# The recurrence's values in one job of 512 columns, attention outputs by way of DRAM, and a first scaling on two engines

## The chip, the core and the metric

The kernel runs on one core of a Trainium2 chip: TensorE (PE) multiplies and writes to PSUM, VectorE (DVE), ScalarE (ACT) and GpSimd (POOL) work element by element, SyncE (SP) issues loads, and each engine runs its own instructions in order, held by semaphores. The metric is the device time of one execution in microseconds, as the median of several runs. The profile is one further execution.

## The reference

One layer of a streaming encoder on x of 1024 tokens x 1024 channels, all in float32:

```
xn = rmsnorm(x, norm1_g);  u = xn @ w_in
q,k,v (8 heads of 64), f,i,q,g (4 heads of 128), gates a,b (1024 each) = split(u)
attention:   w_ts = sigmoid(z_ts) * prod_{s<j<t} (1 - sigmoid(z_tj));   o_sb = w @ v
recurrence:  S_t = diag(f_t) S_{t-1} + k_t i_t^T;  o_t = S_t^T silu(q_t);  o_hg = rmsnorm(o) * silu(g)
merged = sigmoid(a) * (o_sb @ w_o_sb) + sigmoid(b) * (o_hg @ w_o_hg)
h = x + merged @ w_out;  h += relu(rmsnorm(h) @ w_ff1)^2 @ w_ff2;  out = rmsnorm(h)
```

What the change touches are the columns `i` of w_in (512: the values of the recurrence, 128 for each of its four heads), the attention output o_sb, and the scaling inside the first rmsnorm.

## The kernel before

**Two parts for each operand.** Products of float32 accuracy are made of three matmuls (`three`, line 526): each operand is split into a high part (a cast on ScalarE, `hi_copy`, line 143) and a low part (a subtraction on VectorE, `lo_sub`, line 146), and high x high, high x low and low x high are added in PSUM. A weight piece of 128 x 1024 is loaded by SP into one of two buffers with the tag "raw", then split (`Unit.load` and `Unit.split`, lines 435 to 461); the raw buffer comes free with its split. All loads go through SP in one fixed order (`load`, line 128).

**Fill and main.** TensorE's order is written out by two lanes (lines 89 to 118). The main lane holds the attention, and later the recurrence, whose steps depend on VectorE and ScalarE. Between its steps lie steps of "fill": projections out of a stream of jobs (`Stream`, line 471), which need only xn and a weight. A job of a projected head half is 24 matmuls of 512 columns; one step is 6 of them. When a job starts, the weights of the next are split and those of the one after are loaded (`prefetch`, line 490).

**Projections with tokens on the partitions.** The attention's values and the recurrence's values are made by `token_steps` (line 552) from `wide_unit` (line 575): 256 columns of w_in in two pieces of 128 x 1024 (4 k-tiles of 256 columns each), 8 token blocks x 8 k-tiles x 3 matmuls of 256 columns. `i_job(h)` (line 886) makes so the values of heads h and h+1 (`wi0`, `wi2`, PSUM name `pji0`, `pji2`) and ScalarE copies each head's 128 columns out. It is called from `hg_jobs` (line 917) for heads 0 and 2. So the stream holds, behind the last q and k of the attention: f0, q0, i of heads 0 and 1, g0, f1, q1, g1, raw block 0 (gates), f2, q2, i of heads 2 and 3, g2, and so on. For its first job the prefetch is put off to the seventh step and behind a certain cast (`late`, `hi_behind`).

**Attention.** For each head and block of 128 queries: score product `z`, sigmoids on ScalarE, a scan and a product on VectorE (`weights`, line 767), transposes `pw` with their split (`turn`, line 791), and for each pair of blocks the product with v (`values`, line 831, PSUM name `po`), added into `osb`, one SBUF slot of 128 x 1024 for each pair of heads. Of the fill, `n_fill` = 126 steps are spread over it; they end two steps into f1. The four `osb` slots are held from there until the last gate blocks (`raw_job`, line 1276 on), where they are split for the output projection.

**Recurrence.** Heads are treated one after the other by levels: VectorE forms running products of the decay `pp` with `k` and `q`, ScalarE and VectorE split them, TensorE multiplies (`sd`, `sl`), with fill steps between. The rate of fill is a list of constants by stage.

**Start.** `first_norms` (line 596) norms x's first token blocks: ScalarE and VectorE each square half the columns, GpSimd makes the inverse root (line 248), VectorE scales the whole block of 128 x 1024 (line 615), TensorE transposes it (`xnt`) and the first projection `pjqk` begins.

Of the kernel before, what the change touches and what calls it, by code (L numbers as in the profile page):

```python
# [19 lines left out]
P = 128  # L20
# [19 lines left out]
def kernel(  # L40
# [43 lines left out]
    def bank(name):  # L84
        return psum.tile([P, 512], F32, tag="p", name=name)

    class Lane:
        def __init__(self):  # L90
# [458 lines left out]

        return st.add([u for _, u, _ in group], body)  # L550

    def token_steps(name, unit, acts, tbs, epilogue, lo_last=False):

        for tb in tbs:
            ps = bank(f"{name}_{tb}")[:, 0:256]
            for lo in (False, True) if lo_last else (None,):
                for kt in range(KT):
                    sh, sl = acts.stat(kt, tb)
                    wh, wl = unit.hl[kt // 4]
                    cs = slice((kt % 4) * 256, (kt % 4 + 1) * 256)  # L560
# [12 lines left out]
            yield  # L573

    def wide_unit(name, mat, c0):
        return Unit(
            name,
            [
                [
                    (  # L580
                        0,
                        256,
                        mat[k * 512 : (k + 1) * 512, c0 : c0 + 256].rearrange(
                            "(k p) c -> p k c", p=P
                        ),
                    )
                ]
                for k in range(2)
            ],
            wide=True,  # L590
        )
# [4 lines left out]
    def first_norms(tbs):  # L596
        (l, lc), (r, rc) = halves()
        means = {}
        for tb in tbs:
            t, scr = xt[tb], slot(f"n1scr{tb}")  # L600
            ssq = small.tile([P, 1], F32, tag="ssq1", name=f"n1_{tb}_ss", bufs=4)
            in_turn(
                "act",
                nc.scalar.activation(
                    scr[:, lc], t[:, lc], AF.Square, scale=D ** -0.5, accum_out=ssq
                ),
            )
            ms = mean_square(scr[:, rc], t[:, rc], EPS, f"n1_{tb}")
            in_turn("dve", add(ms, ms, ssq))
            means[tb] = inv_root(ms, f"n1_{tb}")  # L610
        for tb in tbs:
            t = xt[tb]
            in_turn(
                "dve",
                nc.vector.tensor_scalar(
                    out=t, in0=t, scalar1=means[tb], scalar2=None, op0=ALU.mult
                ),
            )
            if tb == tbs[0]:
                turn_vectors(0, 1)  # L620
        for part in range(2):
            u_qk0.split(part)
# [168 lines left out]
    def turn(h, qb, between):  # L791
# [36 lines left out]
        seen[h, qc] = seen.get((h, qc), 0) + 1  # L828
        return (h, qc) if seen[h, qc] == 2 else None

    def values(h, qc):
# [25 lines left out]


    hg, ohg = {}, {}
# [23 lines left out]

        return ep

    def i_job(h):
        unit = wide_unit(f"wi{h}", W_IN, C_I + h * P)

        def ep(ps, tb):
            for j in range(2):  # L890
                if tb == 0:
                    hg[h + j, "v"] = slot(f"v{h + j}")
                nc.scalar.copy(hg[h + j, "v"][:, tb * P : (tb + 1) * P], ps[:, j * P : (j + 1) * P])

        unit.late = h == 0

        def body():
            for i, _ in enumerate(token_steps(f"pji{h}", unit, xn, range(NT), ep)):
                yield
                if unit.late and i == 6:  # L900
                    hi_behind[0] = turn_hi[0]
                    st.prefetch()
                    hi_behind[0] = None

        return st.add([unit], body)

    def silu_epilogue(h, key):
        def ep(ps, half):
# [3 lines left out]

        return ep

    j_hg = {}

    def hg_jobs(h):
        for key, c0, ep in (
# [7 lines left out]
            j_hg[h] = proj_jobs([(f"pj{key}{h}", u, ep)], xn)  # L926

    hg_jobs(0)

# [149 lines left out]
    def hg_tail(h):  # L1079
# [5 lines left out]
        for half in range(2):  # L1085
# [67 lines left out]
    class Split:  # L1153
# [15 lines left out]

    a_sb, a_hg = Split("asb"), Split("ahg")  # L1170
    mgs = Acts("ms")
    scratch = ctx.enter_context(
        tc.tile_pool(name="scratch", bufs=1, space=bass.MemoryType.DRAM)
    )

    def dram(name, shape):
        return scratch.tile(shape, F32, tag=name, name=name)

    def half(name, dt=F32):
        return hpool.tile([P, 512], dt, tag="h", name=name)  # L1180

# [74 lines left out]
    def raw_job(cb):  # L1256
# [13 lines left out]
        def body():  # L1270
            p1, p14, g1 = (half(f"{n}_{cb}") for n in ("p1", "p14", "g1"))
            ps, p4 = bank(f"pga{cb}"), bank(f"pgq{cb}")
            if cb >= 6:
                load_g1(cb - 6)
            yield from steps_of(ps, 0, 0, 0, 0, True)
            hi_behind[0] = nc.scalar.copy(p1, ps)
            nc.scalar.dma_start(pd[cb][:, 0, :], p1)
# [11 lines left out]
            (nc.gpsimd if cb < 6 else nc.scalar).dma_start(gd[cb], g1)  # L1289
            if cb >= 4:  # L1290
                a_sb.put(cb - 4, osb[cb - 4])

        return st.add([u], body)

# [86 lines left out]

    j_raw = []
    hg_jobs(1)
    j_raw.append(raw_job(0))
    hg_jobs(2)
    j_raw.append(raw_job(1))
# [777 lines left out]
    for i, it in enumerate(items):  # L2164
# [150 lines left out]
```

## Time and profile before

| | |
|---|---|
| median of 3 runs | 1444.71 us (1444.4 to 1445.86) |
| the profiled execution | 1444.02 us |
| its span in the profile | 1442.2 us |
| TensorE / VectorE / ScalarE / GpSimd busy | 1431.7 / 1105.9 / 664.4 / 142.4 us |

The profile page shows busy time by engine, the span in 40 slices, the DMA queues, the chain of work that ended last, and the costliest groups of instructions. Further views of the same trace are quoted below: the waits of an engine (total us, times, longest), the busy table of chosen windows, the chain inside a window (start us, length us, what), the timeline of an engine (start us, length us, then engine, line, operation), groups by shape (count | busy us, mean ns | idle before), and DMA issues with the median time from issue to landing. Line numbers are those of the kernel before. Matmuls overlap in the trace: the distance from one to the next is its price, not its duration.

### The profile page before, as it was taken

The numbers are of one execution on the slowest core, as the hardware profiler recorded it, in microseconds if no ns is written. First come the engines' busy times: TensorE is split into PE (matmuls) and PEld (weight loads), VectorE is DVE, ScalarE is ACT, GpSimd is POOL, SyncE is SP. The second block draws the span as 40 slices with busy tenths as digits, with TensorE's granted clock in tenths as the row PEclk, the third lists the DMA queues.
The fourth block names the chain that finished last, engine by engine and source line by source line (L and its number), as shares of the span: only waits on it lengthen the run. The fifth ranks groups of instructions, "written<-read, shape, count | busy, mean of one in ns | idle before, by whom it ended". The sixth has DMA issues, their size and how long they took to land.

```text
span 1442.2 us, 19976 instructions
## 1 busy us (share of the span) xinstructions
PE 1431.7 (99%) x7464; PEld 1220.0 (85%) x7464; DVE 1105.9 (77%) x1583; ACT 664.4 (46%) x1150; POOL 142.4 (10%) x338
## 2 busy tenths in 40 slices
PE   9999999999999999999999999999999999999998
PEld 8989988988898888888888888888888888888886
DVE  7699899798747788878778898666666757768765
ACT  7566666652323244432335574444444433523343
POOL 3121121110000012100000300000000000000042
PEclk9999999999999999999999999999999999999999
DMA  7234154321303249655487415344445974776725
GB/s 213 48 98 104 37 96 82 59 44 51 99 21 103 70 134 247 228 177 174 145 292 251 159 46 191 122 144 158 157 150 207 350 262 173 261 276 245 275 100 185
DMA packets 157369, 224.68 MB, mean 156 GB/s; under 512 B 25644, under 2 KB 93784, under 8 KB 157272
## 3 DMA queue, kind: packets, MB, share of 16 engines
q1 hardware_dynamic: 143128, 184.86, 38.0%
q0 software_dynamic: 11264, 33.56, 9.1%
q10 hardware_dynamic: 2880, 4.98, 0.9%
q8 instruction: 59, 0.97, 0.3%
q14 instruction: 38, 0.31, 0.1%
HBM read 162.03 MB, written 61.34 MB: 155 GB/s over the span
## 4 chain that ended last, share of the span: by engine, by line
PE 94%; DVE 3%; issue 1%; ACT 1%; POOL 1%; DMA 0%; SPq 0%; DVEq 0%; POOLq 0%; ACTq 0%
PE pm L121 21%; PE pX L121 9%; PE pW L121 6%; PE pY L121 6%; PE pjqk L121 6%; PE pji L121 3%; PE pys L121 3%; PE pga L121 3%; PE pyh L121 3%; PE gY L121 3%; PE gX L121 3%; PE pjg L121 2%; PE po L121 2%; PE pjv L121 2%; PE z L121 2%; PE pjf L121 2%
## 5 line engine op out<-in xcount | busy, mean ns | idle before, releaser
L144 ACT CAST whid<-w 128x1024 fp32r<-128x1024 f32 x30 | 31.6, 1053 | 152.3 <-PE pm L121 84.4
L777 DVE TENSOR_TENSOR_SCAN rm<-rm,bits 128x511 f32<-128x511 f32 (+7 forms) x72 | 87.3, 1220 | 14.2 <-ACT rm L755 12.7
L121 PE MATMUL pm<-wlod,sh 128*128 128x512 f32 x240 | 93.5, 390 | 0.0
L121 PE MATMUL pm<-whid,sh 128*128 128x512 f32 x240 | 93.4, 389 | 0.0
L121 PE MATMUL pm<-whid,sl 128*128 128x512 f32 x240 | 93.4, 389 | 0.0
L121 PE MATMUL pm<-tl,sh 128*128 128x512 f32 (+1 forms) x210 | 81.3, 387 | 0.0
L121 PE MATMUL pm<-th,sl 128*128 128x512 f32 (+1 forms) x210 | 81.3, 387 | 0.0
L121 PE MATMUL pm<-th,sh 128*128 128x512 f32 (+1 forms) x210 | 81.3, 387 | 0.0
L149 DVE TENSOR_TENSOR wlod<-w,whid 128x1024 fp32r<-128x1024 f32 x30 | 36.7, 1223 | 55.4 <-ACT whid L144 55.4
L149 DVE TENSOR_TENSOR sl<-sa,sh 128x1024 fp32r<-128x1024 f32 x56 | 68.3, 1219 | 1.4 <-ACT sh L144 1.4
L144 ACT CAST wTh<-pw 128x128 fp32r<-128x128 f32 (+3 forms) x96 | 44.4, 487 | 51.0 <-PE pw L124 43.5
L144 ACT CAST sh<-sa 128x1024 fp32r<-128x1024 f32 x56 | 57.3, 1047 | 7.4 <-DMA sa<-ad 7.4
L1957 POOL TENSOR_SCALAR fss<-fss 128x1 f32<-128x1 f32 x8 | 4.5, 560 | 562.2 <-ACT fsc L1952 561.6
L149 DVE TENSOR_TENSOR wTl<-pw,wTh 128x512 fp32r<-128x512 f32 (+3 forms) x96 | 50.8, 548 | 8.7 <-ACT wTh L144 6.0
L121 PEld LDWEIGHTS pm<-wlod,sh 128*128 128x128 f32 x240 | 45.1, 188 | 10.0 <-DVE wlod L149 0.4
L121 PEld LDWEIGHTS pm<-whid,sl 128*128 128x128 f32 x240 | 45.1, 188 | 9.3
L157 DVE TENSOR_TENSOR bt<-bt,rm 128x511 f32<-128x511 f32 (+7 forms) x72 | 48.9, 686 | 5.1 <-ACT bt L758 1.0
L121 PEld LDWEIGHTS pm<-whid,sh 128*128 128x128 f32 x240 | 45.0, 187 | 9.3
L121 PE MATMUL pX<-sql,t1h 128*128 128x512 f32 x128 | 50.0, 391 | 0.1
L121 PE MATMUL pX<-sqh,t1h 128*128 128x512 f32 x128 | 49.9, 389 | 0.0
L121 PE MATMUL pX<-sqh,t1l 128*128 128x512 f32 x128 | 49.8, 389 | 0.0
L755 ACT ACTIVATE rm<-z 128x511 f32<-128x511 f32 (+6 forms) x96 | 47.6, 502 | 4.5 <-DVE bt L157 1.9
(927 smaller groups left out, 4592.0 us busy)
## 6 DMA issues: line engine op xcount, KB each, us to landing
w<-in_w_ff_dram SPq DMA_DIRECT2D x72, 512.0 KB, 5.2
sa<-ad SPq DMA_DIRECT2D x56, 512.0 KB, 6.5
ad<-a SPq DMA_DIRECT2D x32, 256.0 KB, 2.0
ad<-s SPq DMA_DIRECT2D x16, 512.0 KB, 5.5
tw<-in_w_out_dram POOLq DMA_DIRECT2D x24, 256.0 KB, 4.0
x<-in_x_dram SPq DMA_DIRECT2D x8, 512.0 KB, 9.0
xnl<-xnh POOLq DMA_DIRECT2D x8, 512.0 KB, 11.8
pr<-pd SPq DMA_DIRECT2D x8, 512.0 KB, 6.3
```

The costliest lines, as they stand in the source:

```text
L121: return pe(nc.tensor.matmul(*a, **k))
L144: hi_last[0] = after(in_turn("act", nc.scalar.copy(dst, src)), hi_behind[0])
L149: nc.vector.tensor_tensor(out=dst, in0=src, in1=hi.bitcast(F32), op=ALU.subtract),
L157: return nc.vector.tensor_tensor(out=out, in0=a, in1=b, op=ALU.mult)
L755: nc.scalar.activation(rm[:, s0 + c0 - 1 : s0 + m - 1], z[:, c0:m], AF.Sigmoid, scale=-0.125)
L777: sc = nc.vector.tensor_tensor_scan(out=rr, data0=rr, data1=bits[:, 1024 - nk + a : 1024 - nk + b][:, ::-1], initial=rm[:, b : b + 1] if i ...
L1957: nc.gpsimd.tensor_scalar(out=ssq, in0=ssq, scalar1=1.0 / D, scalar2=EPS, op0=ALU.mult, op1=ALU.add)
```

## The change

1. `wide_unit` and `token_steps` take a width n. `i_job()` is called once and makes the values of all four heads: 512 columns, four pieces of 128 x 1024 (2 k-tiles of 512 columns each), matmuls of 512 columns, a step after every second k-tile. It is put behind g1, before raw block 0, and finished before the first state product that needs it (`st.finish(j_i)`). Fill in the attention now ends with q1 (125 steps). The late prefetch is gone.
2. When the last values of a head pair are added, GpSimd stores `osb` to DRAM (`od`) and the slot comes free; gate blocks 4 to 7 load it again through SP. The stores of the gates of blocks 2 to 5 go to ScalarE's queue in place of GpSimd's.
3. Of the first token block, ScalarE scales the right half and VectorE the left.

```diff
-    def token_steps(name, unit, acts, tbs, epilogue, lo_last=False):
+    def token_steps(name, unit, acts, tbs, epilogue, lo_last=False, n=256):
+        pk = 1024 // n
         for tb in tbs:
-            ps = bank(f"{name}_{tb}")[:, 0:256]
+            ps = bank(f"{name}_{tb}")[:, 0:n]
...
-                    wh, wl = unit.hl[kt // 4]
-                    cs = slice((kt % 4) * 256, (kt % 4 + 1) * 256)
+                    wh, wl = unit.hl[kt // pk]
+                    cs = slice((kt % pk) * n, (kt % pk + 1) * n)
                     if lo is None:
                         three(ps, sh, sl, wh[:, cs], wl[:, cs], kt == 0, kt == KT - 1)
-                        if kt == 3:
+                        if kt < KT - 1 and kt % pk == pk - 1:
                             yield
...
         for tb in tbs:
-            t = xt[tb]
+            first = tb == tbs[0]
+            if first:
+                t = xt[tb][:, rc]
+                in_turn("act", nc.scalar.activation(t, t, AF.Copy, scale=means[tb]))
+            t = xt[tb][:, lc] if first else xt[tb]
             in_turn(
                 "dve",
                 nc.vector.tensor_scalar(
                     out=t, in0=t, scalar1=means[tb], scalar2=None, op0=ALU.mult
                 ),
             )
...
+        to_come[h] = to_come.get(h, NT // 2) - 1
+        if r and to_come[h] == 0:
+            od[pair] = dram(f"od{pair}", [P, 1024])
+            nc.gpsimd.dma_start(od[pair], osb.pop(pair))
...
-    def i_job(h):
-        unit = wide_unit(f"wi{h}", W_IN, C_I + h * P)
+    def i_job():
+        unit = wide_unit("wi", W_IN, C_I, HGW)
+        vs = []
         def ep(ps, tb):
-            for j in range(2):
+            for h in range(NHG):
                 if tb == 0:
-                    hg[h + j, "v"] = slot(f"v{h + j}")
-                nc.scalar.copy(hg[h + j, "v"][:, tb * P : (tb + 1) * P], ps[:, j * P : (j + 1) * P])
-        unit.late = h == 0
...
+                    vs.append(slot(f"v{h}"))
+                    hg[h, "v"] = vs[h]
+                nc.scalar.copy(vs[h][:, tb * P : (tb + 1) * P], ps[:, h * P : (h + 1) * P])
+        return st.add([unit], lambda: token_steps("pji", unit, xn, range(NT), ep, n=HGW))
...
-            if key == "g" and h % 2 == 0:
-                i_job(h)
...
+        st.finish(j_i)
         open_block("main")
...
+            if cb >= 4:
+                osb[cb - 4] = slot(f"osr{cb}")
+                load(osb[cb - 4], od[cb - 4])
...
-            (nc.gpsimd if cb < 6 else nc.scalar).dma_start(gd[cb], g1)
+            (nc.gpsimd if cb < 2 else nc.scalar).dma_start(gd[cb], g1)
             if cb >= 4:
-                a_sb.put(cb - 4, osb[cb - 4])
+                a_sb.put(cb - 4, osb.pop(cb - 4))
...
     hg_jobs(1)
+    j_i = i_job()
     j_raw.append(raw_job(0))
...
-    n_fill = 9 * (j_hg[0] - j_qk[0]) + 18
+    n_fill = 9 * (j_q[1] - j_qk[0]) + 9
...
-        st.advance(want - done, j_hg[1])
+        st.advance(want - done, j_q[1])
...
-    st.finish(j_hg[0])
+    st.finish(j_q[1])
```

More of the change, by code (lines that the diff above doesn't have):

```diff
@@ L85, in bank, with dram @@
         return psum.tile([P, 512], F32, tag="p", name=name)
+    scratch = ctx.enter_context(
+        tc.tile_pool(name="scratch", bufs=1, space=bass.MemoryType.DRAM)
+    )
+    def dram(name, shape):
+        return scratch.tile(shape, F32, tag=name, name=name)
     class Lane:
@@ L573, in token_steps, with wide_unit @@
             yield
-    def wide_unit(name, mat, c0):
+    def wide_unit(name, mat, c0, n=256):
+        rows = 1024 // n * P
         return Unit(
@@ L578, in wide_unit @@
             [
[L579 to L588, printed above, removed]
+                [(0, n, mat[r : r + rows, c0 : c0 + n].rearrange("(k p) c -> p k c", p=P))]
+                for r in range(0, D, rows)
             ],
@@ L618, in first_norms @@
             )
-            if tb == tbs[0]:
+            if first:
                 turn_vectors(0, 1)
@@ L829, in turn @@
         return (h, qc) if seen[h, qc] == 2 else None
+    to_come, od = {}, {}
     def values(h, qc):
@@ L884, in f_epilogue @@
         return ep
-    def i_job(h):
-        unit = wide_unit(f"wi{h}", W_IN, C_I + h * P)
+    def i_job():
+        unit = wide_unit("wi", W_IN, C_I, HGW)
+        vs = []
         def ep(ps, tb):
-            for j in range(2):
+            for h in range(NHG):
                 if tb == 0:
-                    hg[h + j, "v"] = slot(f"v{h + j}")
-                nc.scalar.copy(hg[h + j, "v"][:, tb * P : (tb + 1) * P], ps[:, j * P : (j + 1) * P])
-        unit.late = h == 0
[L897 to L905, printed above, removed]
+                    vs.append(slot(f"v{h}"))
+                    hg[h, "v"] = vs[h]
+                nc.scalar.copy(vs[h][:, tb * P : (tb + 1) * P], ps[:, h * P : (h + 1) * P])
+            if tb == NT - 1:
+                vs.clear()
+        return st.add([unit], lambda: token_steps("pji", unit, xn, range(NT), ep, n=HGW))
     def silu_epilogue(h, key):
@@ L913, in silu_epilogue @@
         return ep
-    j_hg = {}
+    j_hg, j_q = {}, {}
     def hg_jobs(h):
@@ L922, in hg_jobs @@
         ):
-            if key == "g" and h % 2 == 0:
-                i_job(h)
             u = cols_unit(f"w{key}{h}", [(W_IN, c0 + h * P, P)])
             j_hg[h] = proj_jobs([(f"pj{key}{h}", u, ep)], xn)
+            if key == "q":
+                j_q[h] = j_hg[h]
     hg_jobs(0)
@@ L1171 @@
     mgs = Acts("ms")
[L1172 to L1177, printed above, removed]
     def half(name, dt=F32):
```

## Prediction

> **What bounds the kernel now.** I read the head of the page first (busy shares, clock, chain), then the waits of TensorE, then the chain and the busy table around the places that the change touches.
>
> ```profile
> span 1442.2 us, 19976 instructions
> ...
> PE 1431.7 (99%) x7464; PEld 1220.0 (85%) x7464; DVE 1105.9 (77%) x1583; ACT 664.4 (46%) x1150; POOL 142.4 (10%) x338
> ...
> PEclk9999999999999999999999999999999999999999
> ...
> PE 94%; DVE 3%; issue 1%; ACT 1%; POOL 1%; DMA 0%; SPq 0%; DVEq 0%; POOLq 0%; ACTq 0%
> ```
>
> TensorE is busy for 99% of the span at an even clock. So the time is the sum of what TensorE streams, plus the few places where it stands still. The waits of TensorE name all that a semaphore explains:
>
> ```profile
> PE warm L121 <- POOL ident masks.py:199: 2.2, 1, 2.2
> PE xnt L124 <- DVE x L615: 0.4, 1, 0.4
> PE pjqk L121 <- DVE xnl L325: 0.3, 1, 0.3
> PE sl L121 <- DVE q L157: 0.2, 1, 0.2
> ```
>
> 2.2 us is the fixed start; 0.7 us are the first rows (touched by the change); 0.2 us is in the recurrence of head 0. A change can therefore win only through fewer streamed columns or through these tenths. It can lose more easily, because TensorE is this full only as long as VectorE keeps up. The busy table (first number behind the window: its length; then PE, PEld, DVE, ACT, POOL, clock, DMA share) shows how near VectorE is:
>
> ```profile
> 200.00:254.00 54.00, 54.00 (x309) 46.64 (x308) 50.18 (x73) 34.51 (x77) 10.98 (x38) 1.00 0.44 85
> 254.00:316.00 62.00, 61.79 (x443) 57.79 (x442) 50.27 (x73) 37.47 (x95) 10.34 (x40) 1.00 0.33 58
> 316.00:358.00 42.00, 41.83 (x246) 34.96 (x245) 39.15 (x92) 10.79 (x17) 0.00 (x0) 1.00 0.14 42
> ```
>
> The end of the attention (254 to 316) leaves VectorE 62.00 - 50.27 = 11.7 us idle; the first recurrence stage (316 to 358) only 2.85 of 42. The chain of waits asked for 314 to 358 says the same: start, length, what.
>
> ```profile
> 313.95 1.13 DVE sd_l L149
> ...
> 330.67 1.13 DVE wg1l L149
> ...
> 342.54 0.35 DVE q L157
> 342.93 2.05 PE sl L121 x16
> ```
>
> For 29 us, from 313.95 to 342.93, the chain is VectorE's own (with short gaps), and TensorE hangs on its last product by 0.2 us. That is the place to price.
>
> **Change 1: one job of 512 columns for two of 256.** Counts: the six groups of 256-column matmuls, of which the first and the last are
>
> ```profile
> L121 PE MATMUL pji<-wi0h,xnh x64: 278/283/288, 254.4 to 290.5; 128*128 128x256 f32 x64
> ...
> L121 PE MATMUL pji<-wi2h,xnl x64: 281/283/287, 393.9 to 422.4; 128*128 128x256 f32 x64
> ```
>
> make 6 x 64 = 384. The changed program has 8 token blocks x 8 k-tiles x 3 products = 192 with 512 columns. The durations in these rows overlap (matmuls are pipelined), so the price is the pitch in the chain, pieces without a gap:
>
> ```profile
> 256.84 2.88 PE pji L121 x24
> ...
> 280.12 0.44 PE pw L124 x4
> ```
>
> ```profile
> 610.94 2.72 PE gX L121 x12
> ```
>
> 2.88 / 24 = 0.120 us for 256 columns, 2.72 / 12 = 0.2267 us for 512. TensorE saves 384 x 0.1198 - 192 x 0.2267 = 46.0 - 43.5 = **-2.45 us**, if nothing makes it wait. The Trainium skill (TensorE: Matmul & The Clock Gate, Back-to-back issue gap) gives an isolated gap of N/2.4 + 2.5 ns; by it the saving would be only 384 x 109.2 - 192 x 215.8 ns = 0.5 us and the time 2 us later. The rows above hold some 13 ns beside N/2.4 at both widths, so they disagree with the page, and the sum goes by the rows.
>
> **What moves with it, end of the attention.** The fill work that covers VectorE's attention work is now g of head 0, then f and q of head 1 (3 x 48 matmuls of 512 columns, 144 x 0.2267 = 32.6 us from 254 on). Before it was the values' first job, g of head 0 and 12 matmuls of f (192 x 0.1198 + 60 x 0.2267 = 36.6 us): 4.0 us less cover. VectorE gets the four scalings after f and the two products after q:
>
> ```profile
> L157 DVE TENSOR_TENSOR g<-pjg,g 128x512 f32<-128x512 f32 x2 | 1.4, 698 | 1.2 <-ACT g L910 1.2
> ...
> L149 DVE TENSOR_TENSOR wg1l<-wg1r,wg1h 128x1024 fp32r<-128x1024 f32 x1 | 1.2, 1231 | 0.0
> ...
> L875 DVE TENSOR_SCALAR pp<-pp,oml,lb 128x512 f32<-128x512 f32 x2 | 1.1, 546 | 0.0
> L872 DVE TENSOR_SCALAR k<-k,oml 128x512 f32<-128x512 f32 x2 | 1.0, 478 | 0.0
> ```
>
> The first row stands for such a product, the second for the split of a weight piece. Two each of 0.546 and 0.478 and two products of 0.7 are 3.4 us more. Its idle time there falls from 11.7 to about 11.7 - 4.0 - 3.4 = 4.3 of 58 us. The window 200 to 254 has the same density (3.8 idle of 54) and TensorE stands at 54.00 of 54.00 in it, so I charge only scattered waits: **+0.3** (0 to 1.5). At the very end a cover goes: the values of block 2 of the last head wait for the transposes "pw" to pass ScalarE (high part) and VectorE (low part). Before, 12 matmuls of f (2.7 us) lay between; now only the four transposes of the next block (0.44 us, above).
>
> ```profile
> 312.42 0.59 ACT L144 CAST wTh<-pw 128x512 fp32r<-128x512 f32 x1 [1.08 <-PE pw L124]
> ```
>
> ```profile
> 313.27 0.68 DVE L149 TENSOR_TENSOR wTl<-pw,wTh 128x512 fp32r<-128x512 f32 x1
> ```
>
> 0.59 + 0.68 - 0.44, and 0.1 for handing over: **+0.9** (0.5 to 1.5). Both engines are free for it by then in the changed order, or it is longer.
>
> **First recurrence stage.** I count from the last score product, which ends where this row starts,
>
> ```profile
> 304.04 0.39 PE L121 MATMUL pjg<-xnh,wg0h 128*128 128x512 f32 x1
> ```
>
> to the product at 342.93. TensorE streams 126 fill matmuls of 512 columns there in both programs (before 18 of head 0's g and 48, 48 and 12 of head 1's f, q and g; after 24 of q, 48 of g and 54 of the values), so its time is the same. VectorE's list changes by: four splits of the values' weights (4 x 1.231), two products after g (2 x 0.7) and the next level's full product (1.2) come; one product, two splits, and the four scalings (0.7 + 2.46 + 2.05) go: 7.5 - 5.2 = 2.3 us more. VectorE was the chain here by 0.2 us, and idle for 2.85 us of its window. So TensorE waits for between 0.2 (the gaps take all) and 2.5 us (they take nothing).
>
> A second chain lies in the same place. The weights come in four pieces through two raw buffers: piece 2 is loaded when piece 0 is split, the following gate weights when piece 2 is split. ScalarE, in order, has the casts of pieces 2 and 3, then the gate weights' cast, then the sigmoid after g, then the cast of level 1. The times of these on ScalarE, and L, the time of one load:
>
> ```profile
> L910 ACT ACTIVATE g<-pjg 128x512 f32<-128x512 f32 x2 | 1.2, 598 | 8.6 <-PE pjg L121 8.6
> ...
> L144 ACT CAST wga0whi<-wga0r 128x1024 fp32r<-128x1024 f32 x1 | 1.0, 1043 | 0.0
> ```
>
> ```profile
> wga0r<-in_w_in_dram SPq DMA_DIRECT2D x1, 512.0 KB, 3.8
> ```
>
> ```profile
> wi0r<-in_w_in_dram SPq DMA_DIRECT2D x2, 512.0 KB, 5.5
> ```
>
> From the last score product: piece 0 split at +11.2 (it takes the place of q's weight split, beside `sd_l`, which ends at 315.08), L, cast and split 2.3, L, cast 1.05, sigmoid 0.6, product 0.7, level 1's product 1.2, its cast 1.0: 18 + 2L. TensorE wants it after 86 fill matmuls and 6 others of 0.2267, 20 of 0.12 and 12 transposes of 0.11, 24.6, and the 0.9 above: +25.5. With L = 3.8, the load of this very stage, where the DMA share is 0.14, it comes at 25.6; with 5.5, measured for the same weights while other loads ran, at 29.0. I take 3.8, by which VectorE's own list sets the stage, and of its 0.2 to 2.5 the middle: **+1.35** (0.2 to 4). What stalls TensorE here gives VectorE time back, so the ring and VectorE's excess don't add.
>
> **What goes.** The 0.2 us at 342.93, and what TensorE loses without a named wait at the old end of the attention (62.00 - 61.79 = 0.2 in the window above), are replaced by the new waits: **-0.4** (-0.4 to 0). In head 1's stage the second 256-column job leaves with its splits; VectorE has room there already, so nothing beyond the count.
>
> **Change 2: attention outputs in DRAM.** Four stores of 512 KB from GpSimd behind the last values of a head pair, four loads on SP at gate blocks 4 to 7. Nothing computes on them until the output projection; the load waits for the store, long past, and for a slot. Behind it on SP are the next gate weights; the splits that follow are VectorE's and ScalarE's. Near the last of them the DMA engines are full:
>
> ```profile
> 550.00:580.00 30.00, 30.00 (x196) 25.36 (x195) 23.89 (x45) 13.73 (x33) 9.50 (x13) 1.00 1.05 286
> ```
>
> 0.5 MB at 286 GB/s is 1.8 us later there for what queues behind; TensorE doesn't stand still in that window. I cost it at **0** (-0.3 to +2). The gate stores of blocks 2 to 5 go to ScalarE's queue, where the later blocks' already are:
>
> ```profile
> 552.15 0.33 ACTq L1289 DMA_DIRECT2D gd<-g  x1
> ```
>
> 4 x 0.33 us in an engine 46% busy: 0 (0 to 0.5).
>
> **Change 3: x0's scaling on two engines.**
>
> ```profile
> 5.53 0.56 POOL L248 TENSOR_TENSOR n_y<-n_ms,expo 128x1 f32<-128x1 f32 x1 [3.19 <-DVE n_ms L1183]
> ...
> 6.69 0.74 DVE L615 TENSOR_SCALAR x<-x,n_y 128x1024 f32<-128x1024 f32 x1
> 6.85 0.99 POOL L248 TENSOR_TENSOR n_y<-n_ms,expo 128x1 f32<-128x1 f32 x1 [0.76 <-DVE n_ms L1183]
> 7.10 0.62 ACT L144 CAST wqk0whi<-wqk0r 128x512 fp32r<-128x512 f32 x1 [0.57 <-DMA wqk0r<-in_w_in_dram]
> ...
> 7.88 0.75 DVE L615 TENSOR_SCALAR x<-x,n_y 128x1024 f32<-128x1024 f32 x1 [0.37 <-POOL n_y L248]
> ...
> 10.28 0.38 PE L121 MATMUL pjqk<-xnh,wqk0whi 128*128 128x256 f32 x1 [0.28 <-DVE xnl L325]
> ```
>
> The second root on GpSimd takes 0.99 instead of 0.56 beside VectorE's scaling and ends with it plus the rest of its own. With half the columns on VectorE (0.48 by the row of `k`) it should end some 0.3 earlier, and x1's scaling and the chain to 10.28 with it; ScalarE's half of x0 fits into its 0.57 idle, but pushes the cast at 7.10 by 0.1 to 0.2. **-0.25** (-0.4 to 0). By the Trainium skill (SBUF — State Buffer, SBUF: two separate sides) the two engines hold a port pair exclusively; then the root gains all that VectorE gives up, at most 0.4.
>
> **Sum** on the profiled execution of 1444.0 (span 1442.2 and 1.8 around it): -2.45 + 0.3 + 0.9 + 1.35 - 0.4 + 0 - 0.25 = -0.55, so 1443.5; the median of the runs, 1444.71 (1444.4 to 1445.86), lies 0.7 above that execution, so the forecast is **1444.2**, a change of nearly nothing. The times below are from the median.
>
> **The rivals.** (a) *The full gain*: VectorE's gaps take in every new wait, as they do from 200 to 254. -2.45 - 0.25 - 0.4 = -3.1: 1441.6. Against it stand the 2.3 us more in a stage whose chain is VectorE already. (b) *Slower: the ring of two raw buffers.* Split, load, split, load, cast, sigmoid stand in series in the first recurrence stage; each us of L costs two. From L = 4.1 on it sets the stage (18 + 2L against 25.5 and some 0.7 of VectorE's), and from 4.6 on the kernel is slower than before: 18 + 9.2 - 25.5 = 1.7, with 0.3, 0.9 and 0.2 that is the 3.1 gained. At 5.5 it is 3.5 + 0.3 + 0.9 + 0.2 - 3.1 = +1.8: 1446.5; at 6.3, +3.4: 1448.1. For it: 5.5 is measured for such weights; against: 3.8 in this stage. (c) *VectorE bounds the attention's end and its excess stays whole*: the upper ends, 1.5 + 1.5 + 2.5 - 3.1 = +2.4: 1447.1. (d) *The outputs' round trip*: a load that waits for its slot holds up SP, and gate weights behind it come late by the 1.8 us above: -0.55 + 1.8 = +1.25: 1446.0. (e) *The change doesn't do what it says*, the pitch per column stays that of 256: no saving, -0.55 + 2.45 = +1.9: 1446.6; the two rows nearly exclude it.
>
> **How the numbers follow.** The forecast with its neighbours 50%, (a) 20%, (b) 13%, (c) 10%, (d) 6%, (e) 1%. A measurement of this kernel can tell about 0.2% (2.9 us) from no change, so "same" is 1441.8 to 1447.6. Three quarters of (a) lie below it and 3 points of what I don't see; of (b) and (c) about half lies above, of (d) a third, and 6 points of what I don't see: faster 0.18, same 0.62, slower 0.20. The range goes down to (a) with its terms at their lower ends (-2.45 - 0.4 - 0.4 - 0.3) and the runs' 0.3, 1440.9, and up to (b) at 6.3, 1448.1.
>
> **What would show it.** 192 matmuls `pji` of 512 columns at 0.2267 pitch, 43.5 us. New rows in TensorE's waits: `po` for VectorE's `wTl` near 1 us, and `sl` for ScalarE or VectorE under 2 us. A cast or split of the values' weights that idles for their DMA shows (b). GpSimd's second root near 0.7 and `pjqk` near 10.0 show the start. From the gate blocks on TensorE's distances equal those of before. I am wrong if TensorE idles in the gate blocks, or if the sum of new waits is under 1 or over 5 us.

## The result and the profile after

The changed kernel takes 1449.91 us (median of 6 runs, 1448.42 to 1451.76), the kernel before beside it 1444.66 (6 runs, 1443.76 to 1445.86): ratio **1.0037** (95% interval 1.0024 to 1.005). The forecast was 1444.2, and 1449.91 lies above its range. The profiled execution of the changed kernel took 1448.85 (span 1447.1), 4.83 more than that of before and 5.35 more than the sum in the prediction (1443.5).

Head of the page, changed kernel:

```profile
span 1447.1 us, 19593 instructions
...
PE 1431.3 (99%) x7272; PEld 1209.7 (84%) x7272; DVE 1105.4 (76%) x1583; ACT 664.9 (46%) x1151; POOL 139.5 (10%) x338
```

The matmuls fell by the 192 counted (7464 to 7272), yet the span grew: so TensorE stands still somewhere. Its waits, as engine, line, what it waited for, then total us, times and longest:

```profile
PE warm L128 <- POOL ident masks.py:199: 2.2, 1, 2.2
PE gX L128 <- DVE gu L1183: 1.9, 1, 1.9
PE sl L128 <- ACT sl_h L151: 1.3, 1, 1.3
PE pga L128 <- ACT p L1279: 1.1, 1, 1.1
PE pX L128 <- DVE a L1183: 0.6, 1, 0.6
PE po L128 <- DVE wTl L156: 0.5, 1, 0.5
PE sl L128 <- DVE q L164: 0.5, 1, 0.5
PE pjqk L128 <- DVE xnl L332: 0.3, 1, 0.3
PE po L128 <- ACT wTh L151: 0.2, 1, 0.2
```

The waits for `sl_h`, `po` and `pjqk` were priced in the prediction. The other four (`pga`, the `sl` for `q`, `gX`, `pX`) lie where it said that nothing changes. Matching TensorE's instructions of both traces one by one shows where the time goes:

| Place | TensorE, changed minus before, us |
|---|---|
| just before the end of the gate blocks (555) | -0.3 |
| 557 to 562: stalls of 1.29, 0.63 and 0.24 | +2.1 |
| second `gX` (620) | +2.1 |
| `pX` (1129) | +0.7 |
| sum | 4.6 of 4.83 |

So up to 555 us the changed kernel was 0.3 us ahead, near the small gain that was forecast, and 4.9 us were lost later, in code that the diff hardly touches.

**First place: the end of the gate blocks.** Chain of waits, changed kernel:

```profile
549.97 5.88 DMA osr<-od
...
556.82 0.58 ACT p L1279
557.40 0.96 ACT wo00h L151
...
559.52 0.68 DVE p L1183
```

The last reloaded output lands at 555.85. Its cast stands on ScalarE ahead of the copy `p` of block 7, and in that order everything behind it waits. ScalarE's timeline shows the wait in brackets:

```profile
555.87 1.04 ACT L151 CAST asbh<-osr 128x1024 fp32r<-128x1024 f32 x1 [4.23 <-DMA osr<-od]
```

In the kernel before, the same casts read a tile in SBUF and wait for nothing:

```profile
549.54 1.99 ACT L144 CAST asbh<-osb 128x1024 fp32r<-128x1024 f32 x2
```

**Second place: `gX`.** ScalarE's timeline, changed kernel, then before:

```profile
576.44 1.05 ACT L151 CAST wo02h<-wo02r 128x1024 fp32r<-128x1024 f32 x1 [6.97 <-DMA wo02r<-in_w_o_sb_dram]
577.39 1.05 ACT L151 CAST gsh<-gs 128x1024 fp32r<-128x1024 f32 x1
```

```profile
573.36 1.05 ACT L144 CAST gsh<-gs 128x1024 fp32r<-128x1024 f32 x1 [5.87 <-DVE gs L1186]
...
576.04 1.05 ACT L144 CAST wo02h<-wo02r 128x1024 fp32r<-128x1024 f32 x1
```

The cast of `wo02` is in no line of the diff, but its place has moved: from behind the cast of `gs` and four squares of `hon` to ahead of them, where ScalarE waits until 576.4 for its weights. (The load itself is hardly later: by the traces' semaphore events it landed 16.7 us after its issue, and 16.4 in the kernel before.) VectorE's timeline shows what comes of that, changed kernel, then before (idle time ahead of an instruction in brackets):

```profile
586.70 0.69 DVE L164 TENSOR_TENSOR hon<-pho,hn_y 128x512 f32<-128x512 f32 x1 [2.33 <-POOL hn_y L250]
...
601.95 1.29 DVE L1186 TENSOR_TENSOR wg0r<-wg0r,wg0r 128x512 f32<-128x512 f32 x2 [1.75 <-DMA wg0r<-in_w_in_dram]
...
611.70 1.22 DVE L156 TENSOR_TENSOR tgl<-wg0r,tgh 128x1024 fp32r<-128x1024 f32 x1
...
619.55 0.68 DVE L1183 TENSOR_TENSOR gu<-pr,gX 128x512 f32<-128x512 f32 x1
```

```profile
599.88 0.68 DVE L1186 TENSOR_TENSOR wg0r<-wg0r,wg0r 128x512 f32<-128x512 f32 x1
603.90 0.69 DVE L1186 TENSOR_TENSOR wg0r<-wg0r,wg0r 128x512 f32<-128x512 f32 x1
606.24 1.22 DVE L149 TENSOR_TENSOR tgl<-wg0r,tgh 128x1024 fp32r<-128x1024 f32 x1
...
613.70 0.69 DVE L1183 TENSOR_TENSOR gu<-pr,gX 128x512 f32<-128x512 f32 x1 [1.38 <-PE gX L121]
```

The second `hon` waits for GpSimd's inverse root `hn_y`, and GpSimd's order has changed too. Its timeline, changed kernel, then before:

```profile
584.67 0.62 POOL L1376 DMA_DIRECT2D yd<-g1r  x1 [2.76 <-DVE g1r L164]
585.36 0.19 POOL L246 TENSOR_SCALAR hss<-hss 128x4 f32<-128x4 f32 x1
585.63 1.03 POOL L250 TENSOR_TENSOR hn_y<-hss,expo 128x4 f32<-128x4 f32 x1
```

```profile
580.83 1.01 POOL L243 TENSOR_TENSOR hn_y<-hss,expo 128x4 f32<-128x4 f32 x1
583.45 0.61 POOL L1373 DMA_DIRECT2D yd<-g1r  x1 [1.62 <-DVE g1r L157]
```

A store of `yd`, which waits for VectorE's `g1r`, now stands ahead of the root and held it for 2.1 us: ScalarE's last sum of squares for it was done at 583.24.

Before, `gu` waits 1.38 us for TensorE: that is VectorE's whole reserve. Afterwards VectorE is late by 5.46 us at `tgl` and 5.85 at `gu`. One step hangs on the next: late `hon`, then the weight differences `wg0r`, which now stand together and wait for their load, then `tgl`, whose end lets the next weights start:

```profile
611.70 1.23 DVE tgl L156
612.95 5.29 DMA wg4r<-in_w_in_dram
...
619.55 0.69 DVE gu L1183
```

TensorE itself is 1.9 us late when it comes to the first `gX` of this stage (stalls at the gates' end), and 4.1 at the second.

### The profile page after: what moved, and what is told of

Read it like the earlier page. It is cut to its first block, busy times and chain, and to the rows that moved or that the text cites. A ratio compares the mean times of both kernels' runs of the same rounds, so it can differ in the third digit from the quotient of the medians.

```text
span 1447.1 us, 19593 instructions
## 1 busy us (share of the span) xinstructions
PE 1431.3 (99%) x7272; PEld 1209.7 (84%) x7272; DVE 1105.4 (76%) x1583; ACT 664.9 (46%) x1151; POOL 139.5 (10%) x338
## 4 chain that ended last, share of the span: by engine, by line
PE 87%; DVE 6%; DMA 3%; issue 2%; ACT 1%; POOL 1%; SPq 0%; DVEq 0%; ACTq 0%; POOLq 0%
PE pm L128 21%; PE pX L128 9%; PE pW L128 6%; PE pjqk L128 6%; PE pY L128 6%; PE pjq L128 3%; PE pjf L128 3%; PE pyh L128 3%; PE gX L128 3%; PE gY L128 3%; PE po L128 2%; PE z L128 2%; PE pjv L128 2%; PE pjg L128 2%; PE pwX L128 2%; PE pji L128 2%
## 5 line engine op out<-in xcount | busy, mean ns | idle before, releaser
L151 ACT CAST wTh<-pw 128x512 fp32r<-128x512 f32 (+2 forms) x96 | 43.9, 486 | 51.3 <-PE pw L131 50.2
L156 DVE TENSOR_TENSOR wTl<-pw,wTh 128x512 fp32r<-128x512 f32 (+2 forms) x96 | 50.6, 548 | 3.9 <-ACT wTh L151 3.2
L760 ACT ACTIVATE rm<-z 128x511 f32<-128x511 f32 (+4 forms) x96 | 48.0, 501 | 3.1 <-PE z L128 1.2
```

The costliest lines, as they stand in the source:

```text
L151: hi_last[0] = after(in_turn("act", nc.scalar.copy(dst, src)), hi_behind[0])
L156: nc.vector.tensor_tensor(out=dst, in0=src, in1=hi.bitcast(F32), op=ALU.subtract),
L760: nc.scalar.activation(rm[:, s0 + c0 - 1 : s0 + m - 1], z[:, c0:m], AF.Sigmoid, scale=-0.125)
```

## The experiments

The first theory (T in the expectations, its parts numbered): the loss is order. An in-order engine holds a cast of data that is loaded late, ahead of work that is ready, at the gates' end (reload of the outputs) and before `gX` (`wo02`, or the sums of `wg0`). Rivals: the DMA traffic of the round trip itself; the four gate stores moved to ScalarE's queue (W); the ring of two raw buffers, rival (b) of the prediction. Ratios are to the kernel before, run on the same chip (medians 1443.99 to 1444.05), with 95% intervals; they go by all runs and not by the medians. Beside the changed kernel itself the kernel before stood at 1444.66, so runs are compared with it by their distance from the kernel before: 5.25 us by the medians for the changed kernel.

**1. H: the changed kernel, with the cast of the last reload behind the copy of block 7.**

```diff
-            hi_behind[0] = nc.scalar.copy(p1, ps)
+            copied = hi_behind[0] = nc.scalar.copy(p1, ps)
...
+                hi_behind[0] = copied
                 a_sb.put(cb - 4, osb.pop(cb - 4))
+                hi_behind[0] = None
```

> The changed kernel with one more order: the cast of the last reloaded attention output (osr of gate block 7) stands behind the copy p of gate block 7 on ScalarE, in place of ahead of it. Its load and all else stay. Theory T (ScalarE's queue is held by a load that lands late, TensorE and VectorE wait behind it): TensorE's wait 'pga for p' of 1.1 us and the 0.6 and 0.2 us behind it go, and, if the 1.9 us of 'gX for gu' 60 us later are VectorE's backlog from the same place, those too: 1449.9 - 4 = about 1446. Rival U (the 1.9 us at gX come from loads that the DMA traffic makes late, not from this place): only 2 us go, 1448. Rival V (the first recurrence stage and the attention's end are the loss): under 1 us changes, 1449 to 1450.

1449.51 us (1445.94 to 1451.16, 5 runs), ratio 1.0032 (1.0019 to 1.0044). In its profiled run, which was its fastest (1445.94), TensorE waits 1.0 us at `gX` and 0.4 at `pga` for `wga6wlo`. The wait for `p` is gone, so this cast made that stall; the median lies 5.5 us above the kernel before, so the time as a whole didn't fall (two of the five runs lie near 1446, three at 1449.5 or more). The stall at the gates' end isn't the larger part of the loss, or what is gained there is given back at `gX`.

**2. B: the reload one block earlier.**

```diff
-            if cb >= 4:
-                osb[cb - 4] = slot(f"osr{cb}")
-                load(osb[cb - 4], od[cb - 4])
+            if 3 <= cb < 7:
+                osb[cb - 3] = slot(f"osr{cb + 1}")
+                load(osb[cb - 3], od[cb - 3])
```

> The changed kernel with each reload of an attention output issued one gate block earlier (blocks 3 to 6 in place of 4 to 7); same traffic, same order of the computing engines but for a few casts near block 7. Theory T: the last output has landed when ScalarE reaches its cast, the waits at the gates' end and at gX go, about 1446. Rival U (traffic): the same bytes, the wait at gX stays, 1448. Rival V: 1449 to 1450.

1449.7 us (1447.17 to 1450.42, 5 runs), ratio 1.0041 (1.0027 to 1.0054). No wait of TensorE for `p` is left, and `gX` waits 3.1 us in place of 1.9: TensorE comes there sooner and stands for longer. The same trade as in H.

**3. D: gate stores of blocks 2 to 5 back on GpSimd** (`cb < 2` to `cb < 6`).

> The changed kernel with the gate stores of blocks 2 to 5 on GpSimd's queue again, all else the same. Theory T: no change beyond 0.5 us, 1449.9, since the reload and not the store's queue is what ScalarE waits for. Rival W (ScalarE's queue issues the stores late and holds ScalarE up, and g1r lands late): 1 to 3 us faster, 1447 to 1449.

1451.16 us (1450.8 to 1451.81, 5 runs), ratio 1.005 (1.0038 to 1.0063): not faster; `pga` still waits 0.9 and `gX` 3.5. The moved stores aren't the cause.

**4. C: four raw buffers for the values' weights** (`unit.roomy = (2, 3)`).

> The changed kernel with pieces 2 and 3 of the values' weights loaded into slots of their own and not through the two raw buffers, so that no load waits for a split in the first recurrence stage. Theory T: only the 1.3 us of 'sl for sl_h' there go, the gates' end stays: 1448.6, within 0.5. Rival V (ring is the loss): 3 us or more faster, under 1447.

1448.88 us (1448.01 to 1451.87, 5 runs), ratio 1.0037 (1.0024 to 1.005). The wait for `sl_h` is gone, `pga` (1.4) and `gX` (2.0) stay, and `pkv` waits 0.7 for `pp`. The ring is real in the trace and small; the time doesn't show it (4.9 us above the kernel before, 5.25 without).

**5. E: the kernel before with its attention outputs kept in DRAM** (change 2's stores and reloads alone; gate stores as before).

> The kernel before with the attention outputs alone sent through DRAM (four stores, four reloads at gate blocks 4 to 7); the values stay in two jobs, the gate stores and the start as before. In its order the cast of the last output stands behind the copy p of gate block 7, and VectorE's order behind the gates is that of before. Theory T2 (it is the instruction order on ScalarE and VectorE around the late loads that costs, not the traffic): within 0.5 us of before, 1444.0 to 1444.5, no wait at gX. Rival U (4 MB more traffic in a full stretch makes the gate weights late): a wait at gX of 1 us or more, 1445.5 to 1448.

1443.84 us (1443.45 to 1452.23, 12 runs), ratio 1.0008 (0.9997 to 1.0018). Nine runs lie within 1443.45 to 1444.18, the others at 1445.72, 1449.41 and 1452.23. So the round trip as such costs nothing that can be told in the usual run, but three runs took 1.7 to 8.2 us more, and none of the 29 of the kernel before beside them went above 1444.88. The profiled one is the slowest, and its chain shows what such a run holds:

```profile
549.68 17.42 DMA wo01r<-in_w_o_sb_dram
...
567.18 1.05 ACT wo01h L151
...
570.78 0.59 ACT pp L1104
```

A weight load took 17.42 us, its cast stood ahead of `pp`, and TensorE waited 5.2 us. It is the same kind of stall at a third place, but here the order is that of the kernel before, and the load is what came late. By the semaphore events of the traces this load, `wo01r`, landed 4.0 to 5.6 us after its issue in the six profiles where no reload is issued just ahead of it (5.6 in the kernel before; N, without reloads, and B and P, with earlier ones, are among them) and 10.1 to 17.4 us after it in the ten with the last reload there. ScalarE's timeline of the changed kernel, then of N:

```profile
562.97 1.05 ACT L151 CAST wo01h<-wo01r 128x1024 fp32r<-128x1024 f32 x1 [3.05 <-DMA wo01r<-in_w_o_sb_dram]
```

```profile
558.93 1.05 ACT L151 CAST wo01h<-wo01r 128x1024 fp32r<-128x1024 f32 x1 [1.99 <-PE pga L128]
```

In the profiles of C and J TensorE waited 0.7 and 1.1 us for `pp` behind that cast. So the traffic isn't free: it makes this load late, and in some runs TensorE pays for it.

**6. J: H, and the differences of `wg0` behind the splits of `ahg` again.**

```diff
-            sub(r1[:, s0], r1[:, s1], r0[:, s0])
+            t = sub(r1[:, s0], r1[:, s1], r0[:, s0])
+            if cb == 0:
+                after(t, put_lo[0])
```

> The changed kernel with two orders pinned: the cast of the last reloaded output behind the copy p of gate block 7 (as in the first experiment), and VectorE's second difference of the gate weights wg0, which waits for a load, behind the splits of the recurrence outputs, where the kernel before has it. Theory T2: the wait at gX, which was 1.2 to 3.6 us in the profiles so far, falls under 0.5, and with it the spread of the runs; 1444 to 1445.5. Rival U: gX still waits 1 us or more, 1447 to 1450.

1450.39 us (1446.53 to 1451.8, 5 runs), ratio 1.0038 (1.0026 to 1.005); `gX` waits 2.8. The differences stand apart again (602.20 and 609.09), so their order isn't what makes `gX` wait: that part of the theory fell.

**7. K: J with the four raw buffers of C.**

> As the one with both orders pinned, and pieces 2 and 3 of the values' weights in slots of their own. Theory T2: 1 us under it, 1443 to 1444.5, so at or a little under the kernel before. Rival U: 1446 to 1449.

1447.26 us (1443.91 to 1450.42, 11 runs), ratio 1.0024 (1.0015 to 1.0033); `gX` waits 2.7. Better, but `gX` is left.

**8. F: the kernel before with the start's scaling shared** (change 3 alone).

> The kernel before with the split of x0's scaling alone. The prediction's term: -0.25 us (-0.4 to 0), so 1443.75 beside 1444.0, with pjqk at about 10.0 in place of 10.28. Rival: ScalarE's half pushes the cast of the first weights and nothing is gained: 1444.0.

1443.76 us (1443.35 to 1445.64, 11 runs), ratio 1.0 (0.9992 to 1.0009). It can't be told from no change by the time.

**9. N: the changed kernel without the reloads** (the output projection reads a tile of normalized input in place of the attention outputs; the stores stay, and so does the order of ScalarE and VectorE).

> The changed kernel without the four reloads: the output projection takes a tile of the normed input in place of the attention outputs (the attention's result is left out of the output); the four stores stay. On ScalarE and VectorE the order behind the gates is that of the changed kernel, among it the early cast of the projection weights wo02, which waits for its load. Theory U (the reloads' 2 MB in the full stretch before 580 make later loads late): no wait at the gates' end nor at gX, 1442.5 to 1444. Theory T3 (the changed order on ScalarE, a cast of wo02 ahead of eight ready instructions, holds VectorE up): the waits at the gates' end go, that at gX stays at 1 us or more, 1445.5 to 1449.

1448.57 us (1448.11 to 1451.71, 5 runs), ratio 1.0035 (1.0023 to 1.0048). Waits of TensorE:

```profile
PE gX L128 <- DVE gu L1183: 2.5, 1, 2.5
```

Without any reload TensorE comes to the first `gX` only 0.1 us later than in the kernel before, the wait for `p` is gone, and `gX` still loses 2.7. So neither the reload's traffic nor the lateness from the gates' end makes that wait. ScalarE's cast of `wo02` is still early, and waits as long (6.99 us):

```profile
574.61 1.05 ACT L151 CAST wo02h<-wo02r 128x1024 fp32r<-128x1024 f32 x1 [6.99 <-DMA wo02r<-in_w_o_sb_dram]
```

**10. L: H, and the cast of `wo02` behind the copy of `ys` that it followed in the kernel before.**

```diff
+                if self.name == "wo02":
+                    hi_behind[0] = ys_copy[0]
...
+                if self.name == "wo02":
+                    hi_behind[0] = None
...
-                        nc.scalar.copy(y, ps)
+                        ys_copy[0] = nc.scalar.copy(y, ps)
```

> The changed kernel with two orders pinned on ScalarE: the cast of the last reloaded output behind the copy p of gate block 7, and the cast of wo02 behind the copy of the second output block, where the kernel before has it. The reloads stay. Theory T3: the wait at gX falls under 0.5, 1444.5 to 1446. Theory U: it stays, 1447 to 1450.

1445.25 us (1443.93 to 1448.84, 11 runs), ratio 1.0008 (0.9999 to 1.0017): 4.3 us less than H by the medians, for the pin of one cast. VectorE's timeline:

```profile
583.33 0.69 DVE L165 TENSOR_TENSOR hon<-pho,hn_y 128x512 f32<-128x512 f32 x1 [0.57 <-POOL hn_y L251]
...
597.97 1.29 DVE L1191 TENSOR_TENSOR wg0r<-wg0r,wg0r 128x512 f32<-128x512 f32 x2 [1.15 <-DMA wg0r<-in_w_in_dram]
...
607.73 1.22 DVE L157 TENSOR_TENSOR tgl<-wg0r,tgh 128x1024 fp32r<-128x1024 f32 x1
...
615.21 0.68 DVE L1188 TENSOR_TENSOR gu<-pr,gX 128x512 f32<-128x512 f32 x1
```

The second `hon` waits 0.57 in place of 2.33, and `gu` stands 4.3 us earlier. TensorE's waits have no row for `gX` any more. The differences of `wg0` still stand together and wait 1.15: with `wo02` in its place that fits into the reserve.

The pin moved more than this cast: on GpSimd the store of `yd` stands behind the second root again (root 582.29, store 583.26). That holds across all sixteen profiles. In the eight in which TensorE waits at `gX` (the changed kernel, H, B, D, C, J, K and N) that store stands ahead of the root and the second `hon` waits 2.33 us; in the other eight it stands behind. So this run doesn't tell the cast's place from the store's, and neither do L_all, R and P below.

**11. L_all: K with the same pin.**

> As the one before, with VectorE's second difference of wg0 pinned too, and pieces 2 and 3 of the values' weights in slots of their own. Theory T3: 1443 to 1444.5. Theory U: 1446 to 1448, as without the pin of wo02 (1447.3).

1444.1 us (1443.08 to 1447.79, 11 runs), ratio 1.0002 (0.9993 to 1.0011).

**12. R: the changed kernel with the pin of `wo02` alone.**

> The changed kernel with one order pinned: ScalarE's cast of wo02 behind the copy of the second output block, as in the kernel before. Theory T3 (that cast makes the wait at gX, the reload's cast makes the waits at 557 to 562): gX waits under 0.5 us, the waits at the gates' end of some 2 us stay, 1446 to 1447.5. Rival (the late reload makes both): gX still waits 1 us or more, 1448 to 1450.

1446.87 us (1445.92 to 1449.57, 11 runs), ratio 1.002 (1.0011 to 1.0029): 2.9 us above the kernel before, 2.4 less than the changed kernel. TensorE's waits have no row for `gX`; the gates' end stays (`pga` waits 1.3 for `p` and 0.8 for `wga6wlo`). One thing goes against reading too much into this profile: TensorE is 3.3 us late at the first `gX` there and 3.7 at the second, so `gX` adds 0.4 (2.1 in the changed kernel), but part of that is that TensorE itself comes later.

**13. Q: the kernel before with `wo02` cast early** (ahead of the same `gs` and the first square of `hon`).

```diff
+                if self.name == "wo02":
+                    early["wo02"] = hi_last[0]
+                    for e in ("gs60", "hon"):
+                        if e in early:
+                            after(early[e], early["wo02"])
```

> The kernel before, nothing of the change in it, with ScalarE's cast of wo02 put ahead of the first head-3 norm squares and the first cast of the gate sums, where the changed kernel has it. Theory T3: gX waits 1 to 4 us for gu, 1446 to 1449, with runs far apart. Rival (the early cast does harm only when the reloads or the later work stand beside it): 1444.0 to 1444.5.

1444.07 us (1443.61 to 1445.32, 11 runs), ratio 1.0001 (0.9992 to 1.001); TensorE has no wait at `gX`. The early cast alone does no harm in the kernel before, though the cast of `gs` behind it runs at 577.20, about as late as in the changed kernel (577.39; 573.36 before). There the differences of `wg0` stand apart (595.4, 597.1, 600.6) and GpSimd's store stands behind the root; `gu` runs at 614.33, 0.63 later than before, and the 1.38 of reserve covers that. So the early cast isn't enough by itself.

**14. P: L_all with the reload one block earlier.**

> All pins and the four raw pieces as before (1444.1), and each reload one gate block earlier; orders of ScalarE and VectorE unchanged by that. If the late reload costs what is left at 537 us (0.8 us) and in the slower runs: 1442.5 to 1443.5, under the kernel before. If not: 1444.

1443.31 us (1442.93 to 1444.02, 11 runs), ratio 0.9996 (0.9987 to 1.0005): 5.9 us less than the changed kernel, and not to be told from the kernel before. Behind the start TensorE waits 0.6 us at `pga` for `wga6wlo` and 0.5 at `po`, and not at `gX`; `wo01r` lands after 4.6 us.

By the distance of the medians from the kernel before, the steps are: changed kernel 5.25, with `wo02` pinned 2.9 (-2.4), with the reload's cast pinned 1.2 (-1.7), with the ring and `wg0`'s order 0.05 (-1.15), with the reload earlier -0.7 (-0.7). The size of a step hangs on the order in which they are taken: the reload's cast alone (H) gave nothing by the median.

## Why the prediction was wrong

1. *192 matmuls at 0.2267.* Right. Chain of waits, changed kernel: 5.47 / 24 = 0.228.

```profile
344.38 5.47 PE pji L128 x24
```

2. *Start, -0.25.* Right: the second root took 0.73 (0.99 before) and `pjqk` began at 9.96 (10.28 before), -0.32. Timeline of the changed kernel:

```profile
6.72 0.73 POOL L255 TENSOR_TENSOR n_y<-n_ms,expo 128x1 f32<-128x1 f32 x1 [0.73 <-DVE n_ms L1183]
...
9.96 0.39 PE L128 MATMUL pjqk<-xnh,wqk0whi 128*128 128x256 f32 x1 [0.26 <-DVE xnl L332]
```

3. *Attention's end, +0.3 and +0.9.* Right within 0.2: 0.23 scattered, and 1.07 at `po`.

4. *First recurrence stage, +1.35.* Right in sum (1.3 for `sl_h` and 0.24 later), and rival (b)'s ring sets it rather than VectorE's list alone: a load takes L = 4.55, above the 4.1 from which the ring was to decide. C took that wait away.

```profile
315.04 4.55 DMA wir<-in_w_in_dram
```

5. ***Change 2, "I cost it at 0 (-0.3 to +2)", with "From the gate blocks on TensorE's distances equal those of before": this step failed.*** The price of the round trip's traffic was about right for the usual run: E's median is that of the kernel before, and N without reloads keeps most of the loss. Its size was not: the load behind the last reload was to come 1.8 us later, and `wo01r` took 11.6 us in place of 5.6, in E's profile 17.4, for which TensorE waited 5.2. What was missed above all is the order. "The splits that follow are VectorE's and ScalarE's" was said of them as if they had no one behind them. Two casts of late data now stood ahead of ready work on ScalarE, one of the reload (2.1 us at the gates' end) and one of `wo02`, and on GpSimd a store stood ahead of a root that VectorE needed (with the cast 2.1 us at `gX`, and more with the clock, below). Rival (d) had half of the first (a load held up by a slot), at +1.25 and 6%, with the harm on SP's queue and not on ScalarE's. What happens at `gX` stood in no rival: it comes from a changed order of instructions that the diff doesn't touch, which the comparison of the two programs' orders would have shown for ScalarE, VectorE and GpSimd. I had read it for the stages around the change only.

6. *The bound "under 1 or over 5 us of new waits".* The new waits of the profiled execution, without the two for the start and `pjqk`, are 1.9 + 1.3 + 1.1 + 0.6 + 0.5 + 0.5 + 0.2 = 6.1, and the prediction named that as what would show it wrong. Its other sign, TensorE idle in the gate blocks, came too (`pga`, 1.1).

Shown by runs: the reload's cast makes the stall for `p` (H, N); the order that comes with the pin of `wo02` takes the wait at `gX` away (L against H, R against the changed kernel); traffic, gate stores and the order of `wg0` alone don't make that wait (N, D, J). **Open**: which step of the order makes it. The early cast of `wo02` isn't enough by itself (Q), and the differences of `wg0` needn't stand together: in J and K they stand apart and `gX` waits 2.8 and 2.7 all the same, in L they stand together and it doesn't wait. What goes with the wait in every profile is GpSimd's store ahead of the second root. No run has the store there with `wo02` in its old place, so the store alone, or the two together, remain. The 0.6 us at `pX` appear in the profile of the changed kernel but not in those of H, N and R, and were not followed.

## What to carry to other kernels

Where engines work in order, a step that turns a tile at hand into a loaded one is priced by who stands behind its first reader, and not by its bytes alone. Compare the order of every engine, GpSimd and its stores too, from the change to the end of the program, not only around it: the cast and the store at `gX` were in no line of the diff. And when one stall is taken away and the time stays, look for the next place where the slower engine's lateness comes due (H and B moved it to `gX`).

## What the runs showed of the hardware

**A stall can cost more than itself.** During the 2.5 us at `gX` in N the clock of TensorE fell. Busy table of N (window, its length, PE, PEld, DVE, ACT, POOL, then clock, DMA share, GB/s):

```profile
618.00:620.00 2.00, 0.99 (x2) 0.83 (x3) 0.96 (x2) 1.60 (x3) 0.00 (x0) 0.64 0.86 350
620.00:622.00 2.00, 2.00 (x6) 1.58 (x5) 1.10 (x1) 1.39 (x2) 0.00 (x0) 0.51 0.41 158
622.00:624.00 2.00, 2.00 (x10) 1.62 (x10) 2.00 (x4) 0.00 (x0) 0.00 (x0) 1.00 0.24 69
```

A clock of 0.64 over the first window and 0.51 over the second is half the clock for 1.44 and 1.96 us: from 618.56, while TensorE stood still (616.50 to 619.01), to 621.96. Six matmuls start in 2 us in place of ten. PE reads "2.00 of 2.00" in both: a busy share doesn't show a slow clock. The second and third matmul behind the wait begin 0.42 us apart:

```profile
619.01 0.80 PE L128 MATMUL gX<-gsh,tgh 128*128 128x512 f32 x1 [2.51 <-DVE gu L1183]
619.61 0.63 PE L128 MATMUL gX<-gsl,tgh 128*128 128x512 f32 x1
620.03 0.63 PE L128 MATMUL gX<-gsh,tgl 128*128 128x512 f32 x1
...
622.08 0.39 PE L128 MATMUL gX<-gsl,tgh 128*128 128x512 f32 x1
```

From 619.01 to 622.08 are seven distances, 3.07 us in place of 7 x 0.227 = 1.59: 1.5 us on top of the wait. The same fall to a half stands in the profiles of K (wait of 2.7), J (2.8) and D (3.5), for 3.4 us each, and of E (5.2), for 6.8 us. But the wait of 3.1 us in B left the clock at 1.00:

```profile
620.00:622.00 2.00, 2.00 (x10) 1.65 (x9) 1.12 (x1) 1.37 (x2) 0.00 (x0) 1.00 0.57 221
```

and so did the 1.9 us in the profiled run of the changed kernel and the 2.0 in C. By the Trainium skill (TensorE: Matmul & The Clock Gate, What's actually happening) the clock is halved after an idle window of some 3.4 us, and the windows run on freely, whatever the kernel does. The traces agree on the length and on the running on: in N the trace's clock record starts with the full clock at 7.56 us; the fall comes 611.0 us later, which is 179 times 3.413, and the full clock is back 3.41 after that. In D, E, J and K too the fall lies a whole number of 3.413 us behind the start of the record. They differ on the idle window, which needn't be idle throughout. With the time cut into stretches of 3.413 us from that start on, the most that TensorE stands still in one stretch is:

| Profile | Wait, us | Most idle time in one stretch, us | Clock |
|---|---|---|---|
| C | 2.0 | 1.62 | 1.00 |
| changed kernel | 1.9 | 1.77 | 1.00 |
| B | 3.1 | 1.80 (1.28 in the next) | 1.00 |
| N | 2.5 | 2.04 | 0.50 |
| K | 2.7 | 2.29 | 0.50 |
| J | 2.8 | 2.59 | 0.50 |
| D | 3.5 | 3.03 | 0.50 |
| E | 5.2 | 3.41 | 0.50 |

So where a wait falls decides: that of B was longer than that of N, but lay across two stretches. In these eight profiles the limit lies between 1.80 and 2.04 us.

Such falls explain part of the spread of the runs. The mean clock of each run is on record: 0.998 or 0.999 in all 86 runs of the kernel before beside the experiments, 0.996 or 0.997 in 25 runs of the others, all of 1447.3 us or more. They aren't all of it: the runs of the changed kernel spread over 3.3 us (those of the kernel before over 2.1 beside them, and 0.7 beside H), and of its slowest three, 1451.76, 1451.48 and 1450.52, only the first shows 0.997.

**Loads near a full DMA share.** From 550 to 580 the DMA share is 1.05 in the kernel before and in the changed one, and 1.03 in E. A load of 512 KB issued at 557.6 (`wo02r`) landed 16.4 us later in the kernel before, and 16.0 to 21.9 us after its issue in the other profiles; one issued at 549.7 (`wo01r` in E) took 17.42 us. The loads of this size that are shown from elsewhere took 3.8 to 5.5. It is this wait, three to four times the usual, that an in-order engine hands on to everything behind it.
